# A residual stream laid out by tokens: row norms, turned blocks, 512 columns of weights as the moving side

## The chip, the cores and the metric

The kernel runs on one core of one Trainium2 chip. The metric is the device time of one execution in microseconds, the median of several. A core has TensorE (PE, matrix products, with its own weight loads shown as PEld), VectorE (DVE), ScalarE (ACT), GpSimd (POOL) and SyncE (SP), which here only issues DMAs. Each engine works its own instructions in order and waits for the others through semaphores.

## The reference

Two residual layers on 512 tokens of 1024 features, all float32: a causal pooling mixer, then a dilated window attention, each followed by a SwiGLU block with 2816 hidden features, and one last norm.

```python
def rmsnorm(x, g):
    xf = x.astype(jnp.float32)
    y = xf * lax.rsqrt(jnp.mean(xf * xf, axis=-1, keepdims=True) + EPS)
    return (y * g.astype(jnp.float32)).astype(x.dtype)

def swiglu(h, w_gate, w_up, w_down):
    g = jnp.einsum('bsd,df->bsf', h, w_gate)
    u = jnp.einsum('bsd,df->bsf', h, w_up)
    return jnp.einsum('bsf,fd->bsd', jax.nn.silu(g) * u, w_down)

for i in range(DEPTH):
    h = rmsnorm(x, norm_mix[i])
    if i % N_MIXERS == 0:
        y = pool_mixer(h, pool_w_in[j], pool_w_group[j], pool_scale[j], pool_w_out[j])
    else:
        y = attn_mixer(h, attn_w_qkv[j], attn_w_out[j])
    x = x + y
    h = rmsnorm(x, norm_ffn[i])
    x = x + swiglu(h, ffn_w_gate[i], ffn_w_up[i], ffn_w_down[i])
return rmsnorm(x, norm_final)
```

## The kernel before

**Three matmuls for one product.** Every float32 operand is split into a high part (rounded to the type that TensorE takes in one pass) and a low part (the rest). A product is `hi*hi + hi*lo + lo*hi`, three matmuls (`mm3`, L193). Weights are split on the way in: `weights` (L101) keeps a queue; SP loads a raw tile of 128 x 1024 (`load`, L87), ACT makes the high part (L118), DVE the low part (L119), some products ahead of use. Raw tiles come from a ring of five (`wraw`) and one of two (`vraw`), split tiles from rings of three and two (and four for the pool input).

**By features.** The stream `x` is held as 8 chunks of 128 features (partitions) by 512 tokens. In every projection but the pool input and two parts of v, the weights are the stationary side and the tokens move. A norm's sum over features is then a sum over partitions: squares are added up on POOL (`Norm`, L232), TensorE sums them in one-column matmuls (`token_sums`, L264), and the inverse root is spread over the partitions by matmuls of ones with diagonals (`spread`, L285). The gain is put on before the projection (`residual`, L321), the inverse root behind it (`rB`).

**Seven products.** Most of the gate and up work and of the down work multiplies 2 x 2 blocks by the seven products of Strassen and Winograd (`seven`, L596), on halves of 256 tokens. A group of four weight tiles (a "quad", two gates and two ups) has seven products of 24 matmuls of 256 columns. Sums of weight blocks are made by DMAs that add into the raw tile (POOL's queue, L98) and by DVE (L114). Of the operands 0 to 6 of a product, 1, 2 and 5 share one `vraw` tile; 1 and 4 are filled by two DMAs, the second one adding. Groups 0 and 1 of each layer are plain: eight projections of 512 columns each, while the inverse root is found and the right sides (`normalise`, `right_sums`, `right_block`) are made for the quads.

**Down.** After groups 0-3, 4-6 (3-5 in pairs of gate and up tiles: `BLOCKS`, L41) and so on, `down` (L650) runs two halves of the output features, seven products each, 126 matmuls of 256 columns a half. PSUM banks `p` and `r` come from rings of two; a half takes one of each, and ACT copies the first three products aside (`keep`, L663) before DVE adds them to `x`. The last two pairs are a plain projection; in layer 1 it is followed, token half by token half, by the final norm (`finish`, L716).

**Order.** TensorE's order is written out by hand (`manual_schedule`, L68); the other engines' order is made by the compiler from the program order and priorities. SP's and POOL's DMA queues are in order, too.

Of the kernel before, what the change touches and what calls it, by code (L numbers as in the profile page):

```python
# [30 lines left out]
R = 4  # L31
J = S // R
SPAN = 36
HEAD = 4
# [8 lines left out]
    [("plain", 0), ("plain", 1)] + [("quad", n) for n in (2, 3)] + [("down", 0)]  # L43
    + [("quad", n) for n in (4, 5, 6)] + [("down", 1)] + [("quad", n) for n in (7, 8, 9)] + [("down", 2)]
    + [("quad", 10)] + [("down", 3)]
)
F_ORDER = [2 * n + m for pairs in BLOCKS for m in range(2) for n in pairs]
TOKENS = np.arange(S).reshape(J, R).T.reshape(-1)


@with_exitstack
def trunk_kernel(ctx: ExitStack, tc: tile.TileContext, xN, xT, gam, consts, ident_d, w0, w1, wv, w_down, outT):
# [11 lines left out]
    wspl = ctx.enter_context(tc.tile_pool(name="wspl", bufs=3))  # L64
# [8 lines left out]

# [4 lines left out]
    SPLITS = {"w": 3, "v": 2, "b": 4}  # L78

    def enqueue(src, shape, kind="w"):  # L80
        queue.append(dict(kind=kind, src=[src], shape=shape))
        return len(queue) - 1

    def live(done, i, kind):
        return sum(queue[n]["kind"] == kind for n in range(i, len(done)))

    def load(item):  # L87
# [6 lines left out]
        if len(shape) == 3:  # L94
            dst = dst.rearrange("p (g c) -> p g c", g=shape[0])
        nc.sync.dma_start(dst, item["src"][0])
# [4 lines left out]
    def weights(i, split_ahead=4, load_ahead=5):  # L101
# [4 lines left out]
        while len(ready) < min(len(raws), i + split_ahead):  # L106
            item = queue[len(ready)]
            kind, shape = item["kind"], item["shape"]
            if len(ready) > i and live(ready, i, kind) == SPLITS[kind]:
                break  # L110
# [4 lines left out]
            pool = pools.get(kind, wspl)  # L115
            hi = pool.tile([P, 1024], F32R, name=kind + "hi")
            lo = pool.tile([P, 1024], F32R, name=kind + "lo")
# [9 lines left out]


    j_in = [[enqueue(w0[0][:, i * S : (i + 1) * S], (1, S)) for i in range(2)] + [enqueue(w0[i], (2, S)) for i in range(1, 4)]]
    j_in.append([enqueue(w0[i], (2, S), "b") for i in range(4, 8)])  # L130
    j_grp, j_out = [enqueue(w0[8], (4, 2 * P))], [enqueue(w0[10 + i], (8, P)) for i in range(2)]
    j_grp.append(enqueue(w0[9], (4, 2 * P)))
    j_out += [enqueue(w0[10 + i], (8, P)) for i in range(2, 8)]

    def enqueue_ffn(layer):
# [3 lines left out]
        def seven(block, n):  # L139

            base = len(queue)
            more = dict(shape=(2, n, P), ahead=8)
            queue.extend([
                dict(kind="w", src=[block(0, 0)], **more),
                dict(kind="v", src=[block(1, 0), block(1, 1)], **more),
                dict(kind="v", into=base + 1, plus=base, **more),
                dict(kind="w", src=[block(0, 1)], **more),
                dict(kind="w", src=[block(0, 0), block(1, 0)], **more),
                dict(kind="v", into=base + 1, plus=base + 3, **more),
                dict(kind="w", src=[block(1, 1)], **more),  # L150
            ])
            return list(range(base, base + 7))

        def quad(n):
            at = layer * 44 + 4 * n
            return seven(lambda m, k: w1[at + 2 * m : at + 2 * m + 2, :, k * 512 : (k + 1) * 512].rearrange("g p c -> p g c"), 4)

        rows = w_down.rearrange("(t p) c -> t p c", p=P)

        def down(half, s, n):  # L160
            at = layer * 8 + 4 * half
            cols = lambda k: slice((s + k * n) * P, (s + (k + 1) * n) * P)
            return seven(lambda m, k: rows[at + m : at + 4 : 2, :, cols(k)].rearrange("g p c -> p g c"), n)
# [34 lines left out]
    def project(ws, hi, lo, ks, ps=None, hooks=None):  # L198
        if ps is None:
            ps = mm.tile([P, S], F32, name="mm")  # L200
# [91 lines left out]
    class InverseRms:  # L292


        def __init__(self, parts):
            self.parts = parts
# [867 lines left out]
```

## Time and profile before

| what | value |
|---|---|
| time, median of 3 runs (1032.86 to 1033.73) | 1033.58 us |
| the profiled execution's own time | 1032.74 us |
| its span, first to last instruction | 1030.9 us |
| granted TensorE clock, mean | 0.994 |
| HBM read, mean rate | 143.61 MB, 141 GB/s |

The span is a little shorter than the time of the same execution, because launching and finishing lie around it. Busy times of an engine are shares of the span; a matmul's duration in a row contains the depth of the pipeline, so the cost of one in a stream is read from start to start. The chain that ended last is followed back from the last instruction, at each step to what released it. A window row gives, for a stretch, each engine's busy time with the count of its instructions, the granted clock, the busy share of the DMA engines and the rate. A group row ends with busy time, the mean duration in ns, and the idle time before with what ended it.

The kernel's stages in the span: pool mixer to 117, FFN of layer 0 to 454, attention to 681, FFN of layer 1 with the last norm to the end.

### The profile page before, as it was taken

The page shows a single profiled execution, that of the slowest core. Times are in us where ns is not written, and L with a number is a line of the kernel's source. Part 1 is how long each engine was busy: PE and PEld are TensorE (multiplying, and loading weights), DVE is VectorE, ACT ScalarE, POOL GpSimd, SP SyncE. Part 2 cuts the span into 40 slices and gives each one's busy share as a digit, 9 for nine tenths or more (in the row PEclk, how much of TensorE's full clock was granted, in tenths as well). Part 3 has the DMA queues.
Part 4 walks back from the last instruction along what each step waited for, and adds up shares of the span by engine and source line. Part 5 has one row for each costly group of instructions (what it writes and reads, how often), then busy time and mean ns, then how long its engine had stood idle before and what let it go on. Part 6 is the DMA issues. An engine that isn't in the chain of part 4 may idle for free.

```text
span 1030.9 us, 17461 instructions
## 1 busy us (share of the span) xinstructions
PE 1016.1 (99%) x7058; PEld 943.0 (91%) x7058; DVE 783.1 (76%) x1061; ACT 522.9 (51%) x800; POOL 159.1 (15%) x131
## 2 busy tenths in 40 slices
PE   9999999999999999999999999999999999999996
PEld 7887889999999999988778899888999999999996
DVE  7436499898887888577888736559989789788844
ACT  7334446555555555452534433444664555455535
POOL 1002100010111101022333200210011110101003
PEclk9999999999999999999999999999999999999998
DMA  8534334688769757432212243424469767966712
GB/s 292 224 84 121 102 103 129 139 214 205 168 150 250 172 133 196 139 116 64 80 58 63 57 131 100 126 82 123 123 158 220 204 147 171 242 148 160 180 39 82
DMA packets 75921, 146.85 MB, mean 142 GB/s; under 512 B 6336, under 2 KB 30016, under 8 KB 75840
## 3 DMA queue, kind: packets, MB, share of 16 engines
q1 hardware_dynamic: 58000, 116.08, 35.6%
q0 software_dynamic: 16320, 28.32, 16.9%
q10 hardware_dynamic: 1520, 1.34, 0.4%
q8 instruction: 55, 0.90, 0.4%
q14 instruction: 26, 0.21, 0.1%
HBM read 143.61 MB, written 2.10 MB: 141 GB/s over the span
## 4 chain that ended last, share of the span: by engine, by line
PE 95%; DVE 2%; ACT 1%; issue 0%; DMA 0%; POOL 0%; ACTq 0%; DVEq 0%; POOLq 0%
PE p L607 30%; PE r L607 15%; PE mm L194 11%; PE mm L196 11%; PE mm L195 10%; PE mm L607 8%; PE mm L269 1%; PE mm L1048 1%; PE mm L1047 1%; PE early L195 1%; PE mm L1049 1%; PE early L194 1%; PE early L196 1%; PE tp L914 1%; PE early L410 1%; DVE h_lo L317 1%
## 5 line engine op out<-in xcount | busy, mean ns | idle before, releaser
L118 ACT CAST whi<-wraw 128x1024 fp32r<-128x1024 f32 (+3 forms) x194 | 189.7, 979 | 257.9 <-PE p L607 103.1
L119 DVE TENSOR_TENSOR wlo<-wraw,whi 128x1024 fp32r<-128x1024 f32 (+3 forms) x194 | 225.7, 1163 | 38.4 <-ACT whi L118 37.5
L119 DVE TENSOR_TENSOR vlo<-vraw,vhi 128x1024 fp32r<-128x1024 f32 (+1 forms) x90 | 100.3, 1116 | 39.7 <-ACT vhi L118 38.5
L118 ACT CAST vhi<-vraw 128x1024 fp32r<-128x1024 f32 (+1 forms) x90 | 86.8, 965 | 76.8 <-PE r L607 56.0
L194 PE MATMUL mm<-h_hi,whi 128*128 128x512 f32 x280 | 112.5, 402 | 0.0
L196 PE MATMUL mm<-h_hi,wlo 128*128 128x512 f32 x280 | 110.2, 393 | 0.0
L195 PE MATMUL mm<-h_lo,whi 128*128 128x512 f32 x280 | 110.1, 393 | 0.0
L607 PE MATMUL p<-t_hi,whi 128*128 128x256 f32 x288 | 81.1, 282 | 0.0
L607 PE MATMUL p<-t_lo,whi 128*128 128x256 f32 x288 | 81.1, 282 | 0.0
L607 PE MATMUL r<-h_hi,vhi 128*128 128x256 f32 x288 | 81.1, 281 | 0.0
L607 PE MATMUL p<-t_hi,wlo 128*128 128x256 f32 x288 | 81.0, 281 | 0.0
L607 PE MATMUL r<-h_hi,vlo 128*128 128x256 f32 x288 | 81.0, 281 | 0.0
L607 PE MATMUL r<-h_lo,vhi 128*128 128x256 f32 x288 | 80.9, 281 | 0.0
L114 DVE TENSOR_TENSOR vraw<-vraw,wraw 128x1024 f32<-128x1024 f32 (+1 forms) x60 | 66.8, 1113 | 0.6
L194 PEld LDWEIGHTS mm<-h_hi,whi 128*128 128x128 f32 x280 | 53.3, 190 | 13.1 <-issue 1.7
L196 PEld LDWEIGHTS mm<-h_hi,wlo 128*128 128x128 f32 x280 | 53.2, 190 | 11.6
L195 PEld LDWEIGHTS mm<-h_lo,whi 128*128 128x128 f32 x280 | 53.3, 190 | 10.5
L607 PE MATMUL p<-u_hi,whi 128*128 128x256 f32 x216 | 61.1, 283 | 0.0
L607 PE MATMUL p<-u_hi,wlo 128*128 128x256 f32 x216 | 61.1, 283 | 0.0
L607 PE MATMUL p<-u_lo,whi 128*128 128x256 f32 x216 | 61.0, 282 | 0.0
L98 POOL DMA_DIRECT2D wraw<-w x18 | 21.8, 1209 | 215.5 <-DVE ct L557 95.5
L607 PEld LDWEIGHTS p<-t_hi,whi 128*128 128x128 f32 x288 | 54.3, 189 | 0.0
(277 smaller groups left out, 3025.0 us busy)
## 6 DMA issues: line engine op xcount, KB each, us to landing
wraw<-w SPq DMA_DIRECT2D x132, 512.0 KB, 3.9
wraw<-w_down SPq DMA_DIRECT2D x48, 384.0 KB, 3.4
vraw<-w SPq DMA_DIRECT2D x18, 512.0 KB, 6.4
vraw<-w POOLq DMA_DIRECT2D x18, 512.0 KB, 6.7
wraw<-w POOLq DMA_DIRECT2D x18, 512.0 KB, 6.6
vraw<-w_down SPq DMA_DIRECT2D x12, 384.0 KB, 4.8
vraw<-w_down POOLq DMA_DIRECT2D x12, 384.0 KB, 5.4
wraw<-w_down POOLq DMA_DIRECT2D x12, 384.0 KB, 7.4
```

What stands on the lines that cost most here:

```text
L98: nc.gpsimd.dma_start(dst, more, accum_op=ALU.add)
L114: nc.vector.tensor_add(raw[:, :n], raw[:, :n], raws[item["plus"]][:, :n])
L118: nc.scalar.copy(hi[:, :n], raw[:, :n])
L119: nc.vector.tensor_sub(lo[:, :n], raw[:, :n], hi[:, :n].bitcast(F32))
L194: nc.tensor.matmul(ps, lhsT=whi, rhs=xhi, start=first, stop=False)
L195: nc.tensor.matmul(ps, lhsT=whi, rhs=xlo, start=False, stop=False)
L196: nc.tensor.matmul(ps, lhsT=wlo, rhs=xhi, start=False, stop=last)
L269: nc.tensor.matmul(cols[:, i : i + 1], lhsT=sq[:, b * P : (b + 1) * P], rhs=ones[:, :1], start=j == 0, stop=j == len(parts) - 1,)
L317: nc.vector.scalar_tensor_tensor(h_lo[:, c, :], xc, gain(i, c), h_hi[:, c, :].bitcast(F32), op0=ALU.mult, op1=ALU.subtract)
L410: mat = lambda o, w, m, **kw: nc.tensor.matmul(o, lhsT=w[:, b, half, cols], rhs=m, skip_group_check=True, **kw)
L607: nc.tensor.matmul(ps[:, g, :], lhsT=w[:, g, c, :], rhs=xx, start=i in (0, 1, 3) and g + c + k == 0, stop=c == n - 1 and k == 2, skip_grou ...
L914: nc.tensor.transpose(tp[:, j, :], todo[i + j], ident)
```

## The change

- **The stream lies by tokens.** `x` is 4 blocks of 128 tokens (partitions) by 1024 features. A norm scales rows: ACT squares with a running sum, DVE finds the inverse root of a block of 128 tokens and scales the block with it and with the gains (broadcast over the partitions by a DMA). TensorE then turns the scaled block, 8 transposes of 128 x 128, and ACT and DVE split it into the high and low parts `h`, by features. The one-column sums and the spreads go.
- **Projections into the stream** (pool out, attention out, down, the last two pairs) have the activations as the stationary side and move 512 columns of weights. Down makes both output halves at once: a product has two token blocks, each in its own `p`, `r` or `mm` bank, and two operand tiles (two pairs and one pair of 128-row tiles); there are no copies aside.
- **Groups 0 and 1 are quads too**, interleaved product by product (`TWO`); token blocks 2 and 3 are turned while the first four products, which need only blocks 0 and 1, run, and their right sides are finished between the later ones (`late`). Group 1 has its own `ct`.
- **One ring of five split tiles** takes the place of the three; a caller that holds several says so (`held`). Loads run ahead 8 (quads), 6 (down) and 5 (the first two groups).
- **Attention** starts with three projections in two halves of the tokens, since blocks 2 and 3 are turned late; no inverse roots are applied behind projections any more. The rotary tables and masks come through POOL's queue into tiles of the norm.
- **The end** scales and stores block by block, the last block in two halves.

```diff
-    wspl = ctx.enter_context(tc.tile_pool(name="wspl", bufs=3))
+    wspl = ctx.enter_context(tc.tile_pool(name="wspl", bufs=5))
...
+        def add(self, b, half):
+            sq = tmp.tile([P, S], F32, name="sq")
+            with tc.high_priority(URGENT):
+                nc.scalar.activation(
+                    sq, x[:, b, COLS[half]], AF.Square, scale=D ** -0.5, accum_out=self.ss[:, b, half : half + 1]
+                )
...
+        def scale(self, b, to, parts):
+            with tc.high_priority(URGENT):
+                r = self.inverse_rms(b)
+                for cs in parts:
+                    nc.vector.scalar_tensor_tensor(to[:, cs], x[:, b, cs], r, self.gain[:, cs], op0=ALU.mult, op1=ALU.mult)
...
+        def turn(self, half, tp):
+            for j in range(4):
+                at = half * S + j * P
+                nc.tensor.transpose(tp[:, j, :], self.xn[:, at : at + P], ident)
...
+    def out_projection(js, where, hi, lo, norm, shift, tps, hook=None):
...
+        four = [mm.tile([P, S], F32, name="mm") for _ in range(4)]
+        for i in range(4):
+            w = weights(js[i])
+            for b in range(4):
+                products(four[b], w, 2 * i, b)
+                if i == 3:
+                    into_stream(b, 0, four[b])
+                    norm.add(b, 0)
+            if i == 0 and hook:
+                hook()
+        ws = [weights(js[4 + i], held=i) for i in range(4)]
+        for b in range(4):
+            ps = mm.tile([P, S], F32, name="mm")
+            for i in range(4):
+                products(ps, ws[i], 2 * i, b)
+            if b in (1, 2):
+                turned(norm, shift, b - 1, tps(), in_order(b - 1))
+            into_stream(b, 1, ps)
+            norm.add(b, 1)
+            if b < 3:
+                norm.prepare(b)
...
+            def down(b):
+                pairs = BLOCKS[b]
+                p, r = ([fps.tile([P, 2, 256], F32, name=t).rearrange("p g c -> p (g c)") for _ in range(2)] for t in "pr")
+                q = [mm.tile([P, S], F32, name="mm") for _ in range(2)]
+                where = (0, 1, 2, 3, 6, 5, 4)
+                target = ((0, 0, 1), (1, 1, -1), (0, 1, 1), (0, 0, 1), (1, 1, -1), (0, 1, 1), (1, 0, -1))
+                for i, acc in enumerate((p, r, p, q, p, r, p)):
+                    ws = [weights(js[i], held=z) for z, js in enumerate(dn[b])]
+                    half, n, sign = target[i]
+                    for t in range(2):
+                        for c, pair in enumerate(pairs):
...
+                                nc.tensor.matmul(
+                                    acc[t], lhsT=u, rhs=w, start=i in (0, 1, 3) and c + k == 0,
+                                    stop=c == len(pairs) - 1 and k == 2, skip_group_check=True,
+                                )
+                        to = x[:, 2 * n + t, COLS[half]]
+                        if sign > 0:
+                            nc.vector.tensor_add(to, acc[t], to)
+                        else:
+                            nc.vector.tensor_sub(to, to, acc[t])
...
+                if kind == "two":
+                    groups = [Group(n, ct_common), Group(n + 1, ct_tile(hn, "ct_second"))]
+                    first_tokens(0, t1r)
+                    for at, (g, i) in enumerate(TWO):
+                        if at in (0, 2):
+                            b = 2 + at // 2
+                            late_banks[b] = [r_tile(), by_four(mm.tile([P, S], F32, name="mm"))]
+                            late(b, "turn")
+                            late(b, 1)
+                            if b == 2:
+                                norm.prepare(3, COLS)
+                        if at == 4:
+                            first_tokens(1, b21r)
+                        if at in (4, 6, 8):
+                            for b in (2, 3):
+                                late(b, at // 2)
+                        groups[g].product(i)
...
+        late(2)
+        norm.prepare(3, COLS)
+        pqk = by_halves(j_qk[:3])
```

`prepare(b)` is `scale` into the tile `xn`, of which there is one. `turned` turns a block and splits both halves of its features; `into_stream` is DVE's addition into `x`; `late(b, 1)` to `late(b, 4)` make the right sides of a block, two or three DVE operations each.

More of the change, by code (lines that the diff above doesn't have):

```diff
@@ L214, in trunk_kernel, with mm3 @@
-    x = stat.tile([P, NC, S], F32, name="x")
-    stat.tile([P, 8], F32, name="gap0")
-    h_hi = stat.tile([P, NC, S], F32R, name="h_hi")
-    h_lo = stat.tile([P, NC, S], F32R, name="h_lo")
-    stat.tile([P, 8], F32, name="gap1")
-    g_sb = stat.tile([P, 6 * NC], F32, name="g_sb")
-    ones = stat.tile([P, P], F32, name="ones")
+    def mm3(ps, whi, wlo, xhi, xlo, first, last, **kw):
+        nc.tensor.matmul(ps, lhsT=whi, rhs=xhi, start=first, stop=False, **kw)
+        nc.tensor.matmul(ps, lhsT=whi, rhs=xlo, start=False, stop=False, **kw)
+        nc.tensor.matmul(ps, lhsT=wlo, rhs=xhi, start=False, stop=last, **kw)
@@ L671, in ffn @@
[L671 to L682 removed]
+                        self.second_half()
```

829 lines of the change are left out of this document (358 added, 471 removed).

## The prediction

> **What bounds the kernel now.** I read the page's busy times and its chain first, then the chain in order of time, then windows by stage.
>
> ```profile
> PE 1016.1 (99%) x7058; PEld 943.0 (91%) x7058; DVE 783.1 (76%) x1061; ACT 522.9 (51%) x800; POOL 159.1 (15%) x131
> ...
> PE 95%; DVE 2%; ACT 1%; issue 0%; DMA 0%; POOL 0%; ACTq 0%; DVEq 0%; POOLq 0%
> ```
>
> TensorE is on the chain for 95% of the span, and nearly nothing waits, so the sum is one of TensorE's issue times: how many matmuls of which width, and what each costs from start to start. Two rows of the timeline, 82 matmuls apart, give the price at 512 columns; the chain gives that at 256.
>
> ```profile
> 9.22 0.39 PE L195 MATMUL early<-wlo,h_hi 128*128 128x512 f32 x1
> ...
> 27.81 0.39 PE L196 MATMUL early<-whi,h_lo 128*128 128x512 f32 x1
> ```
>
> ```profile
> 204.67 2.13 PE r L607 x18
> ...
> 219.71 2.13 PE r L607 x18
> ...
> 255.44 2.85 PE r L607 x24
> ...
> 275.42 2.85 PE r L607 x24
> ```
>
> 18.59/82 = 0.2267 us at 512 columns. From one `r` of `down` to that of the other half are 126 matmuls: 15.04/126 = 0.1194. From one `r` of a quad to the next quad's are 168: 19.98/168 = 0.1189. Two narrow ones cost 0.2388, one wide one 0.2267: a matmul saved by doubling the width is worth 0.012 us. That is the lever of this change, and it is small.
>
> **The sum, part by part.** All against the profiled execution (span 1030.9, whole run 1032.74); the change in it is then put on the median 1033.58, which lies 0.84 above that run.
>
> *Down projections.* Six (three per layer), each 252 matmuls of 256 columns, become 126 of 512: 30.08 to 28.56, six times -1.52 = **-9.1**.
>
> *First two groups of gate and up.* 192 matmuls of 512 (43.53 us) become two quads (39.96): -3.57, twice = **-7.1**.
>
> *Norms on TensorE.* Gone are the one-column sums and the spreads over ones.
>
> ```profile
> 28.20 1.68 PE mm L269 x16
> ...
> 119.01 1.68 PE mm L269 x16
> ...
> 613.00 1.78 PE tp L1005 x16
> ...
> 681.63 1.68 PE mm L269 x16
> ```
>
> ```profile
> 458.95 0.28 PE L269 MATMUL mm<-ones,ssq 128*128 128x1 f32 x2
> ...
> 462.56 0.77 PE L194 MATMUL mm<-h_hi,whi 128*128 128x512 f32 x1
> ```
>
> ```profile
> 463.00:467.00 4.00, 4.00 (x11) 3.03 (x11) 2.63 (x9) 1.87 (x4) 0.00 (x0) 0.50 0.02 6
> ...
> 471.00:475.00 4.00, 4.00 (x20) 3.30 (x19) 2.13 (x5) 1.06 (x1) 2.66 (x2) 1.00 0.00 0
> ```
>
> Kernel start: 1.7. Both FFN starts: 1.68 and four spreads, 0.4, so 4.2 for two. Attention: the sums fill 458.95 to 462.56, 3.6, and 0.4 of spreads; behind them the granted clock is 0.50 (eleven matmuls in 4 us, later twenty), for some 6.8 us, which costs 3.4. Together **-13.3**.
> Added: three norms of 32 transposes, 96 in all. A 128x128 product against the identity takes 1.78/16 = 0.111: **+10.7**. The first three q/k projections go by halves, 144 matmuls of 256 for 72 of 512: 17.1 - 16.3 = **+0.8**.
>
> *The end.* The last projection starts at 995.19 (end of the last quad) and the span ends 35.7 later.
>
> ```profile
> 992.35 2.84 PE p L607 x24
> 995.19 0.23 PE mm L194
> ```
>
> ```profile
> 1022.38 0.17 DVE v L745
> ...
> 1023.57 0.02 issue
> ...
> 1025.91 1.32 DVE x L756 x4
> ```
>
> After: 96 wide matmuls, 21.8; the last one's remainder 0.2; add 0.69, square 0.62 and its accumulator read 0.19; root and polynomial 1.2 (1022.38 to 1023.57); two scalings 1.4; and 3.7 from the last scaling to the end as now (1027.23 to 1030.9); 0.4 for handovers. 30.2, **-5.5**.
>
> ```profile
> L322 DVE TENSOR_TENSOR x<-mm,x 128x512 f32<-128x512 f32 x24 | 16.4, 688 | 37.6 <-PE mm L196 37.6
> ...
> L568 DVE SCALAR_TENSOR_TENSOR hn<-x,g_sb,rB 128x512 f32<-128x512 f32 x16 | 11.1, 743 | 0.0
> ```
>
> ```profile
> L118 ACT CAST whi<-wraw 128x1024 fp32r<-128x1024 f32 x136 | 142.7, 1050 | 187.7 <-PE mm L195 70.2 <-PE p L607 60.2 <-issue 23.1
> ...
> L246 ACT ACTIVATE sq<-x 128x512 f32<-128x512 f32 x24 | 14.7, 618 | 0.0
> ...
> L831 ACT ACTIVATION_READ_ACCUMULATOR e<-e,neg 128x1 f32 x64 | 12.0, 187 | 0.0
> ```
>
> TensorE's own account: -9.1 - 7.1 - 13.3 + 10.7 + 0.8 - 5.5 = **-23.5**.
>
> *Costed at nothing:* the output projections (192 matmuls of 512 before and after, the operands' roles swapped; the pool input already runs so, at 0.2267), the windows (as many matmuls, contiguous now), the copies of v (ScalarE is 51% busy; uncovered, three of 0.6), the four gain rows (512 KB each on SP's queue; uncovered, one landing of some 4 us), and the rotary tables and masks, which move from SP's to POOL's queue and are wanted only after three projections, 17 us on; POOL, 15% busy, loses its additions of squares. At the start, squares now need x by tokens, loaded behind the weights where `bands` stands now:
>
> ```profile
> 25.12 0.42 SPq L376 DMA_DIRECT2D bands<-consts  x1
> ```
>
> If SP's queue stays as full, four loads of 512 KB land some 5 us later than `bands` does, and the windows, now at 40.76, would start up to 4 us late; but the split ring of five and three DVE additions fewer let SP issue earlier. I take 0, keep 0 to 4.
>
> **New waits.** Four places.
>
> *FFN start.* Two interleaved quads run while DVE turns token blocks 2 and 3 into the seven right sides.
>
> ```profile
> 117.00:202.50 85.50, 85.50 (x551) 78.06 (x550) 75.28 (x96) 46.08 (x60) 6.01 (x5) 1.00 0.46 119
> ...
> 232.60:292.50 59.90, 59.90 (x506) 59.90 (x506) 48.66 (x57) 32.65 (x43) 7.28 (x6) 1.00 0.73 176
> 292.50:322.60 30.10, 30.10 (x255) 30.10 (x254) 27.93 (x37) 17.47 (x24) 4.84 (x4) 1.00 0.77 204
> ```
>
> A quad costs DVE 48.66/3 = 16.2. Added are 18 operations of 512 (12.4), two of 1024 (2.5) and one block's scaling (2.2): 49.5 us of DVE in 41.7 of TensorE (39.96 and 16 transposes). With the next two quads it is 81.9 in 81.7, where 75.28 in 85.5 stands now. DVE has no slack until the first down, and the weight splits queue behind the late blocks in it. Bounds 0 and 7.8 per layer; I take 2, as most of the excess (the sums of gate and up) can lag: **+4**.
>
> *Entry of a down.* Its two token blocks take both `p` banks at once; the second was the last quad's, drained by L642 and L643.
>
> ```profile
> 289.69 4.98 PE p L607 x42
> ```
>
> ```profile
> 295.28 0.42 DVE L643 SCALAR_TENSOR_TENSOR ct<-p,ct 128x256 f32<-128x256 f32 x1
> ```
>
> The quad ends at 289.69 + 24 x 0.1189 = 292.54, L643 at 295.70, 3.16 later; the bank is wanted after nine matmuls, 2.04. Bounds 0 and 1.1; I take 0.6, six times: **+3.6**.
>
> *Exit of a down.* Both `vraw` buffers are now held by one down until its sixth product's operands are split (before, its first half gave one back midway). The next quad's accumulated operand starts only then.
>
> ```profile
> vraw<-w SPq DMA_DIRECT2D x18, 512.0 KB, 6.4
> vraw<-w POOLq DMA_DIRECT2D x18, 512.0 KB, 6.7
> ```
>
> ```profile
> L119 DVE TENSOR_TENSOR wlo<-wraw,whi 128x1024 fp32r<-128x1024 f32 x136 | 171.7, 1263 | 25.7 <-ACT whi L118 25.4
> ```
>
> Counted from the down's start: the split's ring slot comes free after product 2, 0.6 + 12.2; splits (0.6, 1.05, 1.26) make 15.7; the two DMAs in turn, with POOL's pick-up 0.7, 13.8: 29.5; splitting 2.3: 31.8. Wanted at 0.6 + 28.56 + 2.86 = 32.0. No margin: SP's queue is in order, every later load stands behind, and DVE is 93% busy. I take 0.4, keep 0 to 5.3, six times: **+2.4**.
>
> *Attention start.* Blocks turn 2.7 us of matmuls apart, about what one block's DVE work takes (scaling 1.4, root 0.8, two low parts 1.4, two additions 1.4): **+1**, 0 to 4.
>
> Sum: -23.5 + 11 = -12.5, so 1033.58 - 12.5 = **1021.1 us**.
>
> [...]
>
> **Rivals.**
> A. *No wait of weight remains*: the scheduler hides all four places: 1010 to 1015. For it: nothing but TensorE waits now. Against: three margins above are under 1 us. Chance 0.16.
> B. *DVE binds the FFN starts and down entries at their upper bounds*: +15.6 and +6.6 in place of 4 and 3.6 make -23.5 + 22.2 + 3.4 = +2.1, 1035.7; seven tenths of the 22.2 make 1029. For it: 49.5 in 41.7. Against: the lag may fall on sums nobody waits for yet. Chance 0.16, half of it under 1031.5.
> C. *Slower: the held v buffers.* If SP's next-quad load waits for the additions in program order, behind product 3's, it starts at 20 instead of 15.7 and the DMAs, beside other loads, take 15 rather than 13.8 (my estimate): 20 + 15 + 2.3 - 32.0 = 5.3 us at each of six exits, +32, so -23.5 + 8.6 of other waits + 32 = +17, about 1050. Turning point: 14.9/6 = 2.5 us per exit, a load begun after 18.4. For it: each load waits for DVE's additions and splits. Against: the compiler's order may put the additions ahead of their place. Chance 0.13, times 1036 to 1060.
> D. *The clock falls.* Rows: 3.6 us of one-column matmuls brought 0.50; the 1.68 us at 119 did not (clock 1.00 from 117). Eight transposes with a wait of over 2 us at one of the three norms would do the same: 3.4 each, at most +10, 1024 to 1031. Chance 0.07. [...]
>
> **Numbers.** Forecast 0.48 (1015 to 1028). About 0.2% either way is what can be told from no change, 1031.5 to 1035.7. Faster 0.16 + 0.48 + 0.07 + 0.08 = 0.79; same 0.07; slower 0.14. Range 1009 to 1034: it leaves out C, the worst of B, the best of A.
>
> **What would show it.** Right: down spans of 28.6 us; two groups in 41 to 44; no L269 rows; clock 1.00 after 460; a tail of 8 us. Wrong: first matmul of a down's second block, or a quad's second product, behind idle time released by DVE or a `vraw` DMA; DVE above 95% after the FFN starts; windows later than 41; a clock of 0.50 beside transposes.

## The result, and the profile after

The changed kernel takes **1111.49 us** (median of 4, 1109.20 to 1113.04) beside 1033.53 for the kernel before: ratio **1.0754**, 95% interval 1.0734 to 1.0773. It is 78 us slower; the forecast was 1021.1, range 1009 to 1034.

The page's busy times, its chain by engine and by line, and the span with the mean clock, of the changed kernel:

```profile
PE 1022.5 (92%) x6582; PEld 928.6 (84%) x6582; DVE 797.3 (72%) x1118; ACT 511.4 (46%) x817; POOL 122.2 (11%) x109
...
PE 70%; DMA 12%; DVE 11%; ACT 3%; issue 3%; POOL 1%; DVEq 0%; ACTq 0%; POOLq 0%; SPq 0%
PE p L555 19%; DMA vraw<-w 8%; PE r L555 8%; PE mm L555 5%; PE mm L200 4%; PE mm L201 4%; PE mm L202 4%; DMA wraw<-w 3%; PE p L639 3%; DVE wlo L123 3%; PE mm L689 3%; PE mm L324 2%; PE mm L326 2%; PE mm L325 2%; PE r L639 2%
```

```profile
core 0: 1109.8 us, clock 0.964
```

TensorE was 95% of the chain before; now it is 70%, and a transfer, `vraw<-w`, holds 8% by itself. The span is 78.9 longer. TensorE is busy 1022.5 - 1016.1 = 6.4 longer, although it has 476 instructions fewer, and not busy 1109.8 - 1022.5 = 87.3 against 1030.9 - 1016.1 = 14.8. So 72.5 of the 78.9 are waits, and the busy part hides a gain under something that makes the same matmuls slower. The view of waits, TensorE alone (who waited for whom: sum, times, longest), says where:

```profile
PE p L555 <- DVE x L647: 40.7, 6, 7.9
PE p L555 <- DVE ct L583: 14.3, 2, 7.2
PE p L639 <- DVE ct L583: 9.3, 6, 1.8
PE p L555 <- ACT ct L569: 3.7, 1, 3.7
PE r L282 <- DVE xn L273: 2.9, 2, 1.7
PE tp L282 <- DVE h_lo L286: 2.5, 1, 2.5
```

The first row is the six exits of a down: the next quad's first product waits for `x` subtractions (L647). The second is the end of each interleaved pair of groups, which the prediction had no term for. The third is the six entries. The chain in order of time (start, duration, what) through the first exit, whose down began at 216.2:

```profile
237.99 0.73 POOL wraw L104
...
239.33 10.80 DMA vraw<-w
...
250.23 1.05 ACT whi L122
...
251.31 1.24 DVE wlo L123
...
252.57 1.23 DVE vraw L119
253.80 0.61 DVE x L647
...
254.54 5.22 PE p L555 x24
```

It reads backwards. The product starts at 254.54 because of a subtraction that ends at 254.4. That subtraction needs only the down's last results, there by 246.88 at the latest, where the row of the down's last matmul ends (timeline of TensorE):

```profile
246.49 0.39 PE L639 MATMUL p<-whi,u_lo 128*128 128x512 f32 x1
254.54 0.55 PE L555 MATMUL p<-h_hi,whi 128*128 128x256 f32 x1 [7.66 <-DVE x L647]
```

In VectorE's own queue (timeline, in brackets the idle time before and what ended it) one sees why it came so late:

```profile
242.84 0.69 DVE L645 TENSOR_TENSOR x<-r,x 128x512 f32<-128x512 f32 x1 [1.03 <-PE r L639]
251.31 1.23 DVE L123 TENSOR_TENSOR wlo<-vraw,whi 128x1024 fp32r<-128x1024 f32 x1 [7.78 <-ACT whi L122]
252.57 1.23 DVE L119 TENSOR_TENSOR vraw<-vraw,wraw 128x1024 f32<-128x1024 f32 x1
253.71 1.28 DVE L647 TENSOR_TENSOR x<-x,p 128x512 f32<-128x512 f32 x2
```

The compiler put the split of the next quad's accumulated operand ahead of the subtractions. The split waits for the cast, the cast for the DMA that lands at 250.13; the queue is in order, so VectorE stands idle for 7.78 us, and the two subtractions behind the split are ready from 246.88 on at the latest. At the end of the interleaved groups the same happens on ScalarE, where `ct`'s activation stands behind a cast that waits for its DMA:

```profile
166.61 1.05 ACT L122 CAST whi<-vraw 128x1024 fp32r<-128x1024 f32 x1 [6.48 <-DMA vraw<-w]
167.56 0.62 ACT L576 ACTIVATE ct<-ct 128x512 f32<-128x512 f32 x1
```

Last, the clock. The product behind the exit took 5.22 for 24 matmuls, where 2.85 was the price. The window around it (stretch, length, busy times, then clock, DMA share, GB/s):

```profile
247.00:259.50 12.50, 4.96 (x24) 4.99 (x25) 8.16 (x8) 3.98 (x4) 0.00 (x0) 0.59 0.47 106
```

So there are three suspects: **B**, two buffers held too long (the load of the next quad's operand starts late); **Q**, the in-order queues that put a drain behind a split; and the two legs of the operand, a load and then an accumulating load. SP's issues show the first begin at 233.07; the second is issued 6.3 later, at 239.33, and takes 10.80.

```profile
233.07 2.71 SPq L102 DMA_DIRECT2D vraw<-w  x2
```

### The profile page after: what moved, and what is told of

It reads as the page before. It is cut to its first block, busy times and chain, and to the rows that moved or that the text cites. A ratio compares the mean times of both kernels' runs of the same rounds, so it can differ in the third digit from the quotient of the medians.

```text
span 1109.8 us, 16591 instructions
## 1 busy us (share of the span) xinstructions
PE 1022.5 (92%) x6582; PEld 928.6 (84%) x6582; DVE 797.3 (72%) x1118; ACT 511.4 (46%) x817; POOL 122.2 (11%) x109
## 3 DMA queue, kind: packets, MB, share of 16 engines
q0 software_dynamic: 17184, 33.36, 17.8%
## 4 chain that ended last, share of the span: by engine, by line
PE 70%; DMA 12%; DVE 11%; ACT 3%; issue 3%; POOL 1%; DVEq 0%; ACTq 0%; POOLq 0%; SPq 0%
PE p L555 19%; DMA vraw<-w 8%; PE r L555 8%; PE mm L555 5%; PE mm L200 4%; PE mm L201 4%; PE mm L202 4%; DMA wraw<-w 3%; PE p L639 3%; DVE wlo L123 3%; PE mm L689 3%; PE mm L324 2%; PE mm L326 2%; PE mm L325 2%; PE r L639 2%
## 5 line engine op out<-in xcount | busy, mean ns | idle before, releaser
L123 DVE TENSOR_TENSOR wlo<-wraw,whi 128x1024 fp32r<-128x1024 f32 (+2 forms) x198 | 228.0, 1157 | 99.5 <-ACT whi L122 94.9
L122 ACT CAST whi<-wraw 128x1024 fp32r<-128x1024 f32 (+2 forms) x198 | 193.0, 980 | 175.2 <-issue 35.6
L122 ACT CAST whi<-vraw 128x1024 fp32r<-128x1024 f32 (+1 forms) x102 | 99.4, 974 | 187.8 <-DMA vraw<-w 75.0
L123 DVE TENSOR_TENSOR wlo<-vraw,whi 128x1024 fp32r<-128x1024 f32 (+1 forms) x102 | 115.0, 1128 | 76.0 <-ACT whi L122 75.8
L555 PE MATMUL p<-h_hi,whi 128*128 128x256 f32 x176 | 57.8, 328 | 55.0 <-DVE x L647 40.7
L555 PEld LDWEIGHTS p<-t_hi,wlo 128*128 128x128 f32 x528 | 100.9, 191 | 0.0
L555 PEld LDWEIGHTS p<-t_lo,whi 128*128 128x128 f32 x528 | 100.9, 191 | 0.0
L555 PE MATMUL r<-h_lo,whi 128*128 128x256 f32 x352 | 99.7, 283 | 0.7 <-DVE h_lo L286 0.7
L555 PE MATMUL r<-h_hi,wlo 128*128 128x256 f32 x352 | 99.6, 283 | 0.0
L555 PE MATMUL r<-h_hi,whi 128*128 128x256 f32 x352 | 99.4, 282 | 0.0
L119 DVE TENSOR_TENSOR vraw<-vraw,wraw 128x1024 f32<-128x1024 f32 x68 | 76.5, 1124 | 0.7
```

Source lines behind the costliest of these rows:

```text
L119: nc.vector.tensor_add(raw[:, :n], raw[:, :n], raws[item["plus"]][:, :n])
L122: nc.scalar.copy(hi[:, :n], raw[:, :n])
L123: nc.vector.tensor_sub(lo[:, :n], raw[:, :n], hi[:, :n].bitcast(F32))
L555: nc.tensor.matmul(ps[:, g, :], lhsT=w[:, g, c, :], rhs=xx[:, c, :], start=i in (0, 1, 3) and g + c + k == 0, stop=c == 3 and k == 2, skip ...
```

## The experiments

Each time stands beside that of the kernel before on the same chip. Rows without an interval (e1 to e8, e13 to e15) are one execution of either kernel. The 1037.39 beside e1 to e8 lies above all 63 other executions of the kernel before on record (1030.30 to 1036.55), so these ratios may be up to 0.4% low. In the runs with an order set, line numbers are 9 or 10 higher.

| run | edit | us | before | ratio (interval) |
|---|---|---|---|---|
| e1_order | order at the exits | 1077.66 | 1037.39 | 1.039 |
| e2_buffer | third `vraw` buffer | 1042.91 | 1037.39 | 1.005 |
| e3_both | both | 1049.74 | 1037.39 | 1.012 |
| e4_order_q | orders, other order of products | 1097.86 | 1037.39 | 1.058 |
| e5_bank | other bank for down | 1071.58 | 1037.39 | 1.033 |
| e6_buffer_bank | buffer, bank | 1035.86 | 1037.39 | 0.999 |
| e7_buffer_bank_v4 | and operand 4 | 1030.72 | 1037.39 | 0.994 |
| e8_plain | second legs left out | 1034.64 | 1037.39 | 0.997 |
| e9_all | e7 and orders | 1030.24 | 1033.15 | 0.9977 (0.9962 to 0.9991) |
| e10_v4_again | e7 in rounds | 1032.95 | 1033.40 | 1.0003 (0.9989 to 1.0018) |
| e11_norm_first | e7, norm first | 1037.46 | 1033.40 | 1.0040 (1.0026 to 1.0055) |
| e12_buffer_again | e2 in rounds | 1042.32 | 1033.40 | 1.0086 (1.0069 to 1.0103) |
| e13_gap_alone | gap 32 bytes less | 1117.00 | 1031.41 | 1.083 |
| e14_gap0 | e7, other gap | 1031.59 | 1031.41 | 1.000 |
| e15_gap3 | e7, third gap | 1041.56 | 1031.41 | 1.010 |
| e16_v4_shift8 | e7, h shifted | 1031.83 | 1032.02 | 1.0001 (0.9986 to 1.0015) |
| e17_all_shift8 | e9, h shifted | 1031.11 | 1032.02 | 0.9987 (0.9971 to 1.0003) |

### The order alone

```diff
+            first_v = item["kind"] == "v" and "src" in item
+            if first_v and gate["shut"]:
+                break
...
+                if first_v:
+                    for ins in gate["after"]:
+                        order.enter_context(tc.issue_after(ins.ins))
...
+                gate.update(shut=False, after=[last])
```

The gate is shut during a down's last two products, and `last` is its last subtraction.

> Only the order of VectorE's work at the six exits of a down is changed: the split of the next group's first accumulated operand is issued behind the down's last two subtractions. Buffers, loads and products stay. Theory Q (the in-order queue holds the subtractions that free the p bank behind a split that waits for its DMA): the first product of the group starts within 1.5 us of the down's last product, and what is left is the operand's own lateness at the second product, 2 to 4 us per exit instead of 5.2 to 8.0 (41.7 in all); the waits fall to 12 to 24 us, the clock stays up at most exits (up to 2.4 us each), and the time to 1065 to 1085 us. Theory B (only the late buffer counts): the same wait moves from the first to the second product, 5 to 8 us per exit, and the time stays at 1100 to 1112 us.

34 us of the 78 went (1111.5 to 1077.7). The view of waits of this run, in part:

```profile
PE p L564 <- DVE ct L592: 11.7, 2, 6.3
PE p L649 <- DVE ct L592: 9.3, 6, 1.7
PE r L564 <- ACT whi L131: 8.8, 4, 4.2
PE p L564 <- ACT ct L578: 5.7, 2, 4.9
...
PE r L564 <- DVE wlo L132: 2.7, 4, 0.8
```

The 40.7 for the subtractions is gone. In its place the *second* product (`r`, operand 1) waits for its own operand, 8.8 + 2.7 = 11.5, at four of the six. So Q is shown for the exits: of 40.7 us, 29 were work held behind a stalled split, and 11.5 are the operand's own lateness. The operand's chain is no faster (the accumulating load of the first exit takes 10.46 here). The entries are as they were (9.3), and the ends of the interleaved groups nearly (11.7 for 14.3), as they should be.

### The third buffer

```diff
-            pools["v"] = open_pool("ffv", 2)
+            pools["v"] = open_pool("ffv", 3)
...
-    stat.tile([P, 40], F32, name="gap1")
+    stat.tile([P, 32], F32, name="gap1")
```

> A third buffer for the accumulated operands, order of the queues left to the scheduler as in the changed kernel (a gap tile of 40 floats is cut to 32 to make room). Theory B (two buffers, both held by a down or by the two interleaved groups, make the next load late): the load starts a whole operand earlier, the six exits lose under 1 us each instead of 41.7 us in all, the two ends of the interleaved groups under 2 us each instead of 14.6, the clock falls behind them go, and the time falls to 1030 to 1050 us. Theory Q alone would also see the wait go, since the split then waits for nothing. Rival M (the accumulating transfers are slow because three or four loads run at once, 10.8 us for the one at the first exit): earlier loads only collide elsewhere, waits turn up within the downs, and the time stays above 1070 us.

> The changed kernel with the third buffer alone, again, in three rounds beside the two above: 12 us over the first of them (1042.91 against 1030.72 in single looks), ratio to before 1.004 to 1.009.

The largest single step: 1111.5 to 1042.9, and 1042.3 in rounds. The exits have no row left among the waits of the repeated run, VectorE runs through the exit, and the clock stays up behind it (0.59 in the window shown above):

```profile
PE p L639 <- DVE ct L583: 9.4, 6, 1.8
PE p L555 <- DVE ct L583: 4.8, 2, 3.2
```

```profile
237.08 1.22 DVE L123 TENSOR_TENSOR wlo<-vraw,whi 128x1024 fp32r<-128x1024 f32 x1
...
240.56 0.69 DVE L647 TENSOR_TENSOR x<-x,p 128x512 f32<-128x512 f32 x1 [0.40 <-PE p L639]
```

```profile
240.40:252.90 12.50, 12.50 (x107) 12.50 (x107) 9.69 (x9) 7.83 (x10) 1.22 (x1) 1.00 0.99 276
```

The order of the queue is still the bad one, split ahead of subtraction, and it costs nothing: the data is there. This run also prices the clock. TensorE's busy time, page of the repeated run:

```profile
PE 1004.7 (97%) x6582; PEld 909.0 (87%) x6582; DVE 796.8 (77%) x1118; ACT 511.4 (49%) x817; POOL 122.1 (12%) x109
```

The same 6582 instructions take 17.8 us less of TensorE than in the changed kernel. Of the 68.8 us of span between them (1109.8 to 1041.0) 51 are waits and 17.8 are matmuls, most of it at clock 0.50 behind the waits: by the clock record of its trace TensorE is busy for 46.8 us at 0.50 in the changed kernel, and the mean clock of the repeated run, 0.991 over 1041.0, leaves at most some 19 there; half of the difference is some 14. The shorter gap, which the third buffer needs, isn't the reason: e13_gap_alone, with the same gap and two buffers, is busy for 1023.5, 18.8 more. Rival M (the loads only collide elsewhere) falls: the accumulating loads into `vraw` still take 9.2 us (median of this run's page; 11.9 for the three of the stretch 200 to 240), and nothing waits for them at an exit.

### Both, and another order of products

The first is the two edits above together. The second has two buffers, the gate also at the end of the interleaved groups, and:

```diff
+QUAD = (0, 3, 1, 2, 4, 5, 6)
...
-                    for i in range(7):
+                    for i in QUAD:
                         group.product(i)
```

> The third buffer and the order of VectorE at the exits together. Theory B: within 5 us of the run with the third buffer alone, since nothing waits for a DMA at an exit any more. Theory Q with late data left over: up to 15 us faster than the run with the buffer alone.

> Two buffers as in the changed kernel. The order at the exits as in the order run, the same gate at the end of the two interleaved groups (the split of the next group's accumulated operand behind the second group's last drain on ScalarE and VectorE), and every later group runs its products in the order 0, 3, 1, 2, 4, 5, 6, so that a product of a plainly loaded operand stands between the first and the one that needs the accumulated operand. Theory Q: the operand is wanted 2.9 us later, so the exits lose under 1.5 us each and the two ends of the interleaved groups under 2 us; waits of 56 us fall to under 15, the clock falls behind them go, and the time to 1035 to 1055 us. Theory B: the wait of 5 to 8 us stays at most exits less the 2.9 us, and the time at 1070 to 1095 us.

Two misses. With the buffer, the forced order costs 6.8 us more than the buffer alone; with two buffers, the other order of products is 20 us slower than the order alone. The view of waits, first of the one, then of the other:

```profile
PE p L564 <- ACT ct L578: 10.6, 5, 5.1
```

```profile
PE p L565 <- ACT ct L579: 41.2, 19, 5.0
```

One reason for both: after product 2, ScalarE copies `p` aside before product 4 may add to it. In the order 0 to 6, product 3 stands between and covers the copy; in 0, 3, 1, 2, 4 nothing does, and it stalls at every one of the 18 quads that run by themselves (the other of the 19 times is in the interleaved groups, 5.0). In the first run 5.1 of the 10.6 are in the interleaved groups, where the run with the buffer alone has the same wait once (5.1); the other 5.5 are new, and I read their cause from the waits alone, so it isn't shown: the splits held back come to lie in front of the same copy. At the exits no row is left in the first run and some 2 us in the second (1.3 and 0.8 at one exit), so the theory of the exit held, and the edit broke a cover elsewhere.

### Which bank, and the two legs

```diff
-                p, r = ([fps.tile(...) for _ in range(2)] for t in "pr")
-                q = [mm.tile([P, S], F32, name="mm") for _ in range(2)]
+                p, r = ([fps.tile(...) for _ in range(n)] for t, n in zip("pr", (1, 2)))
+                p, *q = p + [mm.tile([P, S], F32, name="mm") for _ in range(3)]
+                p = [p, q.pop(0)]
```

> Two buffers for the accumulated operands and the scheduler's order, as in the changed kernel; but a down takes the p bank of its second block from the mm pool (three of its four banks instead of two), so that neither the last group's product at its entry nor the down's last subtraction at its exit has a p bank that the next work needs. Theory Q: with no bank to hold, the order of VectorE at the exits does not matter, the exits come out as in the order run (0.4 to 5.1 us, 14 us in all), the six entries (1.4 to 1.9 us, 10.3 in all) go to under 0.3 us each, the ends of the two interleaved groups stay (5 to 7 us each); time 1060 to 1075 us, some 10 under the order run. If the exits lose 5 to 8 us each as before, it was not the bank that the first product waited for, and the time is 1090 to 1102 us.

> The third buffer and the down's second p bank from the mm pool. The entries (10.5 us in the run with the buffer alone) go, nothing else: 1030 to 1035 us. If the entries are bound by the drain of the last product's results for the down itself (its left operands) and not by the bank, the wait moves to the second product and the time stays at 1038 to 1043 us.

Without a shared `p` bank the entries' row is gone from both runs, 9.3 us, and a down runs its 28.6 us without a gap (a window of e10_v4_again, which has this edit, stands further down). e6 came out 0.9 above its expected 1030 to 1035. With two buffers the exits lose 18.2 (11.5 + 4.5 + 2.2 in its waits, none of them for L647), some 7 more than in the order run, most of it at ScalarE's copy of `p` (`keep`) behind casts. Two of the three rows:

```profile
PE p L555 <- ACT keep L565: 11.5, 6, 1.9
PE r L555 <- DVE wlo L123: 4.5, 6, 0.8
```

```diff
         nc.sync.dma_start(dst, item["src"][0])
-        for more in item["src"][1:]:
-            nc.gpsimd.dma_start(dst, more, accum_op=ALU.add)
```

> Two buffers and the scheduler's order, as in the changed kernel; the second, accumulating load of every summed operand is left out, so the operands hold one part of their sum only. Theory A (the two legs in a row, 5 us and then 10 us, make the operand late): the operand at the exits is there some 10 us earlier, the exits lose under 1 us each and the time falls to 1030 to 1050 us. Theory H (the hold of the two buffers alone, or the load's place in the queue, makes it late): the exits still lose 3 us or more each and the time stays above 1070 us.

With two buffers and the bad order, but one leg (the kernel leaves out the second part of every sum), the exits wait for nothing. So three things make the wait together: a load that starts half-way through a down, two legs of together 17.1, and a queue that lets the split go first. An earlier load or a single leg removes it whole; the order alone takes 29 of the 40.7. (Leaving the second legs out also takes their transfers off the DMA queues; the runs do not part the two.)

### What was left: FFN starts, and a gap that was not empty

```diff
-            item = dict(kind="v" if i in (1, 2, 5) else "w", ...)
+            item = dict(kind="v" if i in (1, 2, 5) or i == 4 and wide else "w", ...)
...
-                    quad(n + g, i, 5)
+                    quad(n + g, i, 5, g == 1)
```

> As the run with buffer and bank, and the second interleaved group's operand 4, the sum of two loads, takes one of the three buffers for accumulated operands instead of a wraw buffer. In the run with the third buffer TensorE waits 5.2 us in the first FFN (at 143.79 us) for a copy on ScalarE that stands behind the split of this operand, whose second load started at 137.9 because four of five wraw buffers were held by operands 0 and 3 of both groups. If that is the cause the wait goes to under 1.5 us and the clock fall behind it too: 5 to 8 us under the run with buffer and bank, 1022 to 1030 us. Rival: the third buffer is then missing at the next group, where 2 to 5 us turn up in each FFN; then it stands within 2 us of that run or above it.

> The kernel of the run with buffer, bank and operand 4 (1030.72 us beside 1037.39 of before in one look) again, in five rounds on one chip with the next. Ratio to before 0.990 to 0.997. If its single look was luck, 0.997 to 1.001.

The next run has three orders more: priority for the drain of a group's last product, the block part wanted later behind the norm, and the gate on the splits of the first operands. The one after it has only the second of them.

```diff
+                        with tc.high_priority(URGENT):
                             nc.scalar.activation(ct[:, 1, 0, 0, :], p[:, 0, :], AF.Silu, scale=-1.0)
...
-                            first_tokens(1, b21r)
+                            with tc.issue_after(xn.ins):
+                                first_tokens(1, b21r)
```

> As the run with buffer, bank and the second group's operand 4 in an accumulated buffer (1030.72 us), and the order of the in-order queues is set at two places more: the drain of a group's last product goes ahead of the splits on ScalarE and VectorE; at the start of each FFN the sum of block parts that is wanted later goes behind the last norm, and the splits of the first two accumulated operands go behind the second turned block's work. What is left of waits at these places in that run is 1.35, 1.69, 1.22 and 1.89 us at the FFN starts and 2.31 and 1.50 us at the ends of the interleaved groups, 10 us in all. Theory Q: most of it goes, 1019 to 1026 us. If these waits are the data's own (the norm's chain, the second load), the time stays at 1028 to 1031 us.

> That kernel, and at the start of each FFN only the last norm goes first: the block parts that are wanted later and the second turned block's later steps are issued behind it on VectorE; the splits stay where the scheduler puts them. In the run with all orders set the splits of the first accumulated operands came later and the first interleaved groups took 90.6 us instead of 89.3, while those of the second FFN took 83.2 instead of 84.5. Theory Q: the waits for the last norm (1.35 and 1.89 us) go and nothing comes back: 2 to 3 us under the kernel above. Rival: they come back one product later, within 1 us of it.

With operand 4 of the second interleaved group in a `v` buffer, the wait for ScalarE's copy (L569, 3.7 in the changed kernel, 5.4 in e6) has no row any more, and e7 is 5.1 us under e6, near the 5.4 that went. Both are single executions, and the twelve of e7's kernel in e10 lie 7 us apart (1029.9 to 1036.9), so only the missing row shows the gain. In rounds this kernel is level with the one before, 1.0003, so the 0.994 of the single pair doesn't hold. What it still waits for:

```profile
PE p L555 <- DVE ct L583: 5.3, 2, 3.9
PE r L282 <- DVE xn L273: 2.9, 2, 1.7
PE tp L282 <- DVE h_lo L286: 2.5, 1, 2.5
PE p L555 <- ACT keep L565: 1.8, 3, 1.1
```

Setting orders by hand at these places (e9) brought at most 2 to 3 us, not the 5 to 12 expected: the wait for the norm goes in both FFNs, but in the first one others of 1.1, 0.8 and 0.7 for split operands stand a few products later. With only the norm put first it is slower (1.0040), where 2 to 3 us less than in e10 were expected. The version with all orders is the best of the study, 0.9977, a gain at the edge of what can be told; with `h` shifted (e17, below) the same orders give 0.9987, with 1 inside the interval.

In the runs with the gap cut to 32 floats (e10, e12, e13 and e16), the 512-column products of `h` were slower, 0.233 from start to start for 0.227. One line of the kernel grouped (count, min/median/max ns, first and last start): the changed kernel, e12_buffer_again, then e14_gap0.

```profile
L200 PE MATMUL early<-whi,h_hi x14: 389/389/389, 20.0 to 28.9; 128*128 128x512 f32 x14
```

```profile
L200 PE MATMUL early<-whi,h_hi x12: 395/396/396, 19.7 to 27.4; 128*128 128x512 f32 x12
```

```profile
L200 PE MATMUL early<-whi,h_hi x11: 389/389/389, 20.1 to 26.9; 128*128 128x512 f32 x11
```

The next three cut 8 floats from one gap each: `gap1` (behind `h`, two buffers), `gap0` (ahead of `h`) and `gap3` (behind the `t` tiles).

```diff
-    stat.tile([P, 32], F32, name="gap0")
+    stat.tile([P, 24], F32, name="gap0")
```

> The changed kernel, two buffers, with only the gap tile behind the h tiles cut from 40 to 32 floats, as in all runs with a third buffer. In those runs the 512-column products of h against weights started 0.234 us apart in place of 0.227, and the 256-column ones 0.117 in place of 0.119. Theory S (the shift of 32 bytes between h and the weights' tiles does it): the same rates here, +3 to +4 us and -2.5 us, so the time within 3 us of the changed kernel's 1111.5. Theory N (the third buffer, or the denser work, does it): 0.227 and 0.119 here.

> The kernel of the repeated run with buffer, bank and operand 4, with the 32 bytes taken from the gap ahead of the h tiles, so that h and the weights' tiles keep their distance and both move. The order of every engine's instructions is the same. Theory S by distance: 0.227 and 0.119 as in the changed kernel, time within 2 us of 1030 to 1033. Theory S by the place itself: 0.234 or another rate.

> The same, with the 32 bytes taken from the gap behind the t tiles of the FFN, so that only the u tiles move against h and the weights. Theory S: the products of h stay at 0.227 and 0.119; the downs, which use u, may go from 0.227 to 0.234 (756 such matmuls, +5 us) and the time to 1030 to 1037, or stay, and the time is within 2 us of 1030 to 1033.

The gap alone, with two buffers, gives the slow rate too (395/396/396 in the same view), so the third buffer is not its cause. (Its time, 1117.0, is above what was expected; the exits lost 42.6 in that execution.) Taken ahead of `h`, so that `h` and the weights keep their distance, the 32 bytes cost nothing, at an unchanged order of instructions. Taken behind the `t` tiles, only `u` moves against the weights, and now the downs are slower, as one of the two expected outcomes had it, 29.40 against 28.60 (e10_v4_again, then e15_gap3):

```profile
206.80:235.40 28.60, 28.60 (x128) 23.67 (x127) 26.59 (x36) 13.12 (x16) 4.54 (x4) 1.00 0.73 204
```

```profile
208.00:237.40 29.40, 29.40 (x129) 23.62 (x128) 26.53 (x36) 13.25 (x16) 4.54 (x4) 1.00 0.69 196
```

That is 0.8/126 = 6 ns a matmul, as above. The run took 1041.56, above the 1037 expected: the six downs make 4.8, the last pairs, which use `u` too, 1.2 (192 matmuls at 0.233 for 0.227), and in this one execution the mean clock over the span was 0.989 for 0.995 in e10, some 13 us more at 0.50, which is up to 6. For the time of e2 and e12 the matter is small: averaged over all 3696, the narrow products of the FFN go from 0.1192 to 0.1184 with the same cut (not to the 0.117 of the expectation), which gains back the 3 us that 624 wide ones lose.

```diff
-        h_hi, h_lo = tokens_at(0)
+        h_hi, h_lo = tokens_at(8)
```

(at both places, and where blocks are turned for the attention)

> The kernel of the repeated run with buffer, bank and operand 4 (gap behind h at 32 floats), with h of the pool mixer and of the attention placed 8 floats further on, so that its distance to the weights' tiles is again that of the changed kernel, while the FFN's h stays where it is. Theory S: 512-column products of h back at 0.227, 256-column ones of the FFN still at 0.117, TensorE busy some 4 us less than in that run (1001.4), time 2 to 5 us under it, ratio to before 0.994 to 0.998. If the place of h alone decides, the rates stay or others appear.

> The same with the run that sets the order at both FFN starts and at the drains (ratio 0.9977 without the shift): ratio to before 0.992 to 0.996.

Putting `h` itself back at the old distance worked in one place only. In the attention the products of `h` go from 0.233 from start to start (e10) to 0.229, beside 0.228 in the changed kernel; in the pool mixer they stay at 0.233 (393/398/398 in the view above, where the changed kernel has 0.227). The times did not move beyond their spread, against the 2 to 5 us expected. So the distance between two operands matters, but is not the whole rule; the rest stays open.

## Why the prediction failed, step by step

- **Downs, 30.08 to 28.56**: right. 28.60 with no idle, once nothing shares a bank, so six save 8.9 for the 9.1 forecast.
- **The end, 30.2**: right. 1079.3 to the end of the span, 30.5.
- **TensorE's own account, -23.5**: right within about 5 us. 1030.9 - 23.5 = 1007.4; the four waits of e10_v4_again shown make 12.5, smaller new ones some 5, that is 1025; its span is 1029.0. The other 4 are not placed.
- **Exit of a down**: this is the step that failed. It said "I take 0.4, keep 0 to 5.3, six times: +2.4". Measured: 40.7 of waits, 6.8 each, beyond the end of the bounds too, and most of the 17.8 of lost clock. Three parts of it. The load's start was well forecast: 15.7 after the down's start, and it was 233.07 - 216.2 = 16.9, about 1 of it from an entry longer than assumed. The two legs were mis-sized: 13.8 was taken from medians of the kernel before, 233.07 to 250.13 is 17.1 (the first with POOL's pick-up 6.3 for 7.1, the second 10.8 for 6.7); a split ending at 252.55 and wanted at about 249.6 is 3.0 late, and the order run shows 2.2 at this exit and 11.5/6 = 1.9 on the mean. And the step assumed that a late operand stalls the product that uses it. It stalled the product before, by 7.7, because the drain of that product's bank was queued behind the split. The step spoke of SP's in-order queue and of a busy VectorE, but did not ask what stands behind a waiting split on VectorE; that is the gap in the working.
- **The turning point of rival C** (a load begun after 18.4) was wrong for the same reason: the load began earlier, and the kernel was slower than C's 1050 all the same. C had the right place and too small a price (5.3 for 6.8, and the clock on top).
- **Entry of a down, 0.6 each**: mechanism right, size off: 9.3/6 = 1.55, above its bound of 1.1. The drain L583 stood behind another split in VectorE's queue and the two operations after it, not only behind ScalarE's L642 (L582 here):

```profile
217.46 1.22 DVE L123 TENSOR_TENSOR wlo<-vraw,whi 128x1024 fp32r<-128x1024 f32 x1
...
219.53 0.42 DVE L583 SCALAR_TENSOR_TENSOR ct<-p,ct 128x256 f32<-128x256 f32 x1
```

- **FFN starts, +4**: 3.7 + 2.9 = 6.6, inside the bounds. **Ends of the interleaved groups**: 14.3, no term at all; the text looked for exits at downs alone, while two groups side by side also hold both buffers.
- **Attention start, +1**: 2.5.
- **The clock** (rival D) was asked at the transposes, at most 10. One fall, 3.4 us long, did come there, behind the transposes at 501.42; most came behind the long waits. Over the span it was some 80 us at 0.50, (1 - 0.964) x 2 x 1109.8, where before it was 12.

Sum: 1007.4, waits 73.4 as shown in the view, and 17.8 of clock make 1098.6 of 1109.8; the smaller waits, some 3, close part of the rest, and about 8 is not placed.

## What to carry over

When an operand becomes late, look at each engine that prepares it and ask what stands behind it in that engine's queue: here the price was paid by the oldest drain that was stuck (40.7 us at the six exits), not by the operand's own user. A ring of buffers is counted by how long one user holds it: two buffers that one stage takes both of are no double buffering across that stage's end, and a bound worked out from medians of transfers should be widened by what the same transfer takes while others run (here the two legs took 17.1 us for the 13.8 worked out). A gain of 1% in matmul shape is worth making only if the same count of buffers and banks still lets the next stage start early; here the shape was right and the repaired kernel is still only level with the old one.

## What the hardware did that was not expected

- **An accumulating transfer was slow beside others of its kind.** DMA issues on the page of the changed kernel, then those of the stretch 229 to 256 alone (count, size, median us from issue to landing); the kernel before had 6.7 on its page for the first of these rows, and 6.4 for the second.

```profile
vraw<-w POOLq DMA_DIRECT2D x22, 512.0 KB, 9.7
vraw<-w SPq DMA_DIRECT2D x22, 512.0 KB, 5.1
```

```profile
vraw<-w POOLq DMA_DIRECT2D x2, 512.0 KB, 11.4
wraw<-w POOLq DMA_DIRECT2D x1, 512.0 KB, 9.5
```

  In the same stretch the kernel before has three such transfers too, 7.9, 8.2 and 7.9, but issued 7 us and more apart (230.64, 240.84, 247.73); here they are issued at 237.99, 239.33 and 240.61. That their overlap makes them slow is argued from this; no run varies it alone.

- **32 bytes between two operand tiles changed a matmul's rate**, 389 to 396 ns and 0.227 to 0.233 us from start to start at 512 columns, and the other way at 256 columns, 0.119 to 0.118 (the 0.117 and 0.234 of the expectations lie near the medians). The rates are averages over some hundred matmuls of the same form at full clock.
- **The clock did not fall after every like wait.** The same eight transposes behind the same wait, in the changed kernel and in e10_v4_again: once at clock 0.50 (0.50 from 501.70 to 505.10), once at the full rate (the products of 256 columns behind them start 0.117 apart, for 0.21 in the changed kernel).

```profile
501.42 1.78 PE L282 MATMUL tp<-ident,xn 128*128 128x128 f32 x8 [2.55 <-DVE h_lo L286]
```

```profile
459.76 1.09 PE L282 MATMUL tp<-ident,xn 128*128 128x128 f32 x8 [2.55 <-DVE h_lo L286]
```

In the changed kernel six exits and two ends, with waits of 5 to 8 us, each had a stretch at 0.50 with them: it began within the wait at seven of the eight and 0.24 us behind it at the last exit (wait to 1057.80, 0.50 from 1058.04), and lasted 2.9 to 5.9 us past the wait's end. In the clock record of this trace the eleven stretches at 0.50 that end within the span last 3.41, 6.83 or 10.24 us, and all begin on one grid of 3.41 us. The wait of 2.55 us ahead of the transposes, 498.87 to 501.42, lies whole in one step of that grid, 498.26 to 501.67, and the fall came with the next step. Why the same wait left the clock up in e10_v4_again isn't shown.
